# Gate products, rotation, weight splits and gate maxima moved in a hybrid encoder layer

## The chip, the cores and the metric

The kernel runs on one core of a Trainium2 chip. A core has a matrix engine (TensorE, "PE" in the profile, its weight loads "PEld"), VectorE ("DVE"), ScalarE ("ACT"), GpSimd ("POOL") and SyncE ("SP", which here only issues DMAs). Each engine takes its instructions strictly in the order in which they were put into its queue; engines wait for each other through semaphores. TensorE writes only to PSUM, eight banks of 128 x 512 float32; the other engines copy results out of a bank ("evict" it) before TensorE can use it again. GpSimd does not read PSUM in this kernel. The metric is the device time of one execution in microseconds (us), lower is better.

## The reference, cut to what matters

Two sequences (prompt and sample) of 512 tokens with 1024 channels go through one layer with the same weights, in float32:

```python
x = x + 0.5 * swiglu(rms_norm(x), w_gate, w_up, w_down)        # FFN 1, 2816 hidden columns
proj = rms_norm(x) @ w_in                                      # q, k, v, mq, mk, mv, gates, ...
aq, ak = rope(rms_norm(aq)), rope(rms_norm(ak))                # 8 query heads, 2 key heads of 64
att = softmax(aq @ ak.T / 8) @ av
mem = sigmoid(o_pre) * head_norm(mlstm_fwd + mlstm_bwd)        # 4 heads of 128, two directions
x = x + (sigmoid(g_att) * (att @ w_up_att) + sigmoid(g_mlstm) * (mem @ w_up_mlstm)) @ w_out
x = x + 0.5 * swiglu(rms_norm(x), ...)                         # FFN 2, then a final norm

swiglu = (silu(x @ w_gate) * (x @ w_up)) @ w_down
rope:    out[0::2], out[1::2] = x0 * c - x1 * s, x0 * s + x1 * c
mlstm:   D[t, s] = cumsum(f)[t] - cumsum(f)[s] + i[s]          # for s up to t
         m[t] = max(running term, max over s of D[t, s]);  weights exp(D - m);  1 / max(|den|, exp(-m))
```

The mLSTM needs, for each head, direction and block of 128 tokens, the maximum of a gate row: once with a triangular mask added (over s up to t) and once without it (over a whole block). Those maxima fix the scales of all exponentials of the head.

## The kernel before, in words

**Float32 by parts.** Every float32 operand of a matmul is split into a high part (a ScalarE copy, rounded to the format that TensorE takes at full rate) and a low part (a VectorE subtraction, original minus high). A product is then three matmuls: high x high, high x low, low x high. For weights, `fetch_w` issues the DMA into one of four raw buffers (`wr`) and `split_w` (L218 to L223) makes the two parts in one of four buffers (`w8`). `load_w` (L225) is both in a row; it serves the mixing layers.

**FFN, gate and up.** Gate and up weights of 128 hidden columns (a block) and the two sequences form a 2 x 2 by 2 x 2 block product, done with seven products instead of eight; each is twelve matmuls of 512 columns (`product`, L293). There are 22 blocks per FFN. Products accumulate into shared PSUM banks, and sums of them give gate and up of both sequences. `gu_first` does the two products that need only one sequence. For seven blocks it runs ahead and its results are parked in DRAM (`kept`); these blocks later need five products. The order of the blocks alternates a parked with a fresh one for fourteen blocks, then eight fresh ones follow. `gu_rest` (L315 to L347) does the rest of a block: VectorE and ScalarE evict the banks Y and Z (L326, L330, L334, L339, L344), ScalarE applies Silu (L312, L341), and in the last two lines the two products gate x up are formed (L345, L346), on GpSimd. Evictions carry `shifted(SOONER)`. `Sides` (L349 to L378) makes from the results of two blocks the seven right-hand sides of the down projection: splits on ScalarE (L358) and VectorE (L359), differences on VectorE (L365, L372, L374, L376), and two DMAs to DRAM for each (L360, L361). It carries `shifted(LATER)`.

**FFN, down.** `ffn_down` does 28 steps of matmuls (L541) over those sides. The change does not touch it.

**Mixing.** `mix` runs once per sequence. `tok_proj` and `proj` are products with weight slices, each with its own `load_w`; `go` keeps one unit loaded ahead of the one computed. A unit of `proj` is 24 matmuls of 512 columns and one eviction. In order:
1. keys, values and gate columns; then queries.
2. `gates` makes the gate rows and writes them to DRAM (`ebuf`); small columns per block go to `cs`.
3. `rope_apply` (L737 to L758) norms and rotates the keys once and the queries in four blocks: the normed tile times the cosine table on GpSimd (L750), the swapped halves times the sine table on VectorE (L755), the sum on VectorE (L757). `q_rope` splits and transposes the result (L885).
4. Attention, a loop over eight heads: scores and softmax (`scores`, L904, with VectorE's maximum L913, reciprocal L916 and scaling L917 and ScalarE's exponential L915), transposes and product with the values (`attend`, L921), and after each head one or two projection units from `queue` (`fill`).
5. Four mLSTM heads (`mem_head`, L1010, and `mem_out`, L1080), with the value projection (96 matmuls) between the first `mem_head` and its `mem_out` and projection units between the others.
6. Gates, merge and output projection (L1118 to L1138).

In `mem_head`, for each direction, a DMA spreads a gate row from DRAM over all partitions (L1018), GpSimd adds the mask (L1022), VectorE takes the two maxima (L1023, L1024); small VectorE work and one exponential make the scales (L1027 to L1039); then ScalarE makes 20 exponentials of 128 columns (L1061) from the rows with and without mask, and VectorE multiplies them with the scores (L1063). The rows live in four slots (tag `eb`, two per direction), taken in turn.

**Who orders the work.** A planner at compile time turns the program into one queue per engine. Each instruction has a number, its place in the program; among those that the planner takes to be ready by its own estimate of times, the lowest number goes first. `shifted(n)` adds n to the numbers in its block, so a negative n lets them go ahead of earlier code. On the chip the order is fixed: an instruction that waits holds up all behind it on its engine.

Of the kernel before, what the change touches and what calls it, by code (L numbers as in the profile page):

```python
# [8 lines left out]
F32 = mybir.dt.float32  # L9
# [17 lines left out]
def encoder(ctx, tc, I, outs):  # L27
# [14 lines left out]
    def nm(s):  # L42
        n_id[0] += 1
        return f"{s}_{n_id[0]}"
# [173 lines left out]
    def split_w(raw, lo_eng, pin=lambda i: i):  # L218
# [3 lines left out]
        pin(lo_eng.tensor_tensor(lo, raw, f(hi), op=ALU.subtract))  # L222
        return hi, lo  # L223

    def load_w(view, lo_eng):  # L225

        return split_w(fetch_w(view), lo_eng)

# [84 lines left out]
    def gu_rest(W, xc, got, ring, mid):  # L315
# [26 lines left out]
        product(Y, W[T4], xc[T4], False)  # L342
        with shifted(SOONER):
            V_.tensor_tensor(v1, v1, Y, op=ALU.add)  # L344
        G_.tensor_tensor(g0, g0, v1, op=ALU.mult)  # L345
        G_.tensor_tensor(u2, u2, v5, op=ALU.mult)  # L346
        return g0, u2  # L347

    class Sides:  # L349
# [360 lines left out]
    def mix(s, xh, xl, early=None, extra=None, after=None):  # L710
# [4 lines left out]
        def fill(n):  # L715
            go(*queue[:n])
            del queue[:n]
# [19 lines left out]
        def rope_apply(t, rq, tab, bsel):  # L737
# [9 lines left out]
                             rq.unsqueeze(2).to_broadcast([P, 8, DA]), op=ALU.mult)  # L747
            o, m = T2(), T2()
            v4 = lambda x: x.rearrange("p (b h e) -> p b h e", b=nb, e=DA)
            G_.tensor_tensor(v4(o), v4(n), cb, op=ALU.mult)  # L750
            v5 = lambda x: x.rearrange("p (b h i two) -> p b h i two", b=nb, h=hn_, two=2)
            s4 = sb.rearrange("p b (i two) -> p b i two", two=2)
            for bb in range(nb):
# [143 lines left out]
            q_rope(b)  # L897
        go(mem_qk(0, 1), mem_qk(1, 0), mem_qk(1, 1))


        att = A([P, 4, 2, S], F32R, "att")
        afs = {}
# [57 lines left out]
        for h in range(HA):  # L960
            nxt = scores(h + 1) if h + 1 < HA else None
            attend(h, Ps)
            Ps = nxt
            fill(1 if h < 4 else 2)
            if h == 2 and extra:
                extra()
        fill(99)


# [39 lines left out]

        def mem_head(h):  # L1010
            qk = qks[h]
            ebs, ems = [], []
            st = small(64, "st")
            pm_, bm, Mx, mm_, bd, n1, n2, en = [st[:, 8 * i:8 * i + 8].rearrange("p (d b) -> p d b", d=2)
                                               for i in range(8)]
            for d in range(2):
                eb = T2(F32, "eb")
                nc.sync.dma_start(eb, ebuf[d, h:h + 1, :].rearrange("a s -> (a s)").partition_broadcast(P))  # L1018
                em = T2(F32, "eb")
                eb3 = eb.rearrange("p (b s) -> p b s", b=4)  # L1020
                em3 = em.rearrange("p (b s) -> p b s", b=4)
                G_.tensor_tensor(em3, eb3, tabs[3][:, d].unsqueeze(1).to_broadcast([P, 4, P]), op=ALU.add)  # L1022
                V_.tensor_reduce(pm_[:, d], em3, axis=AX.X, op=ALU.max)  # L1023
                V_.tensor_reduce(bm[:, d], eb3, axis=AX.X, op=ALU.max)  # L1024
                ebs.append(eb3)
                ems.append(em3)
            a_, x_, B_ = csv[:, 0, :, :, h], csv[:, 1, :, :, h], csv[:, 2, :, :, h]  # L1027
            V_.memset(Mx[:, :, 0], 0.0)
            for i in range(3):
                V_.tensor_tensor(Mx[:, :, i + 1], Mx[:, :, i], B_[:, :, i], op=ALU.add)  # L1030
                V_.tensor_tensor(Mx[:, :, i + 1], Mx[:, :, i + 1], bm[:, :, i], op=ALU.max)
            V_.tensor_tensor(mm_, a_, Mx, op=ALU.add)
            V_.tensor_tensor(en, pm_, x_, op=ALU.subtract)
            V_.tensor_tensor(mm_, mm_, en, op=ALU.max)
            V_.scalar_tensor_tensor(bd, x_, -1.0, mm_, op0=ALU.mult, op1=ALU.subtract)
            V_.tensor_tensor(n1, a_, mm_, op=ALU.subtract)
            V_.tensor_tensor(n2[:, :, 2:4], n1[:, :, 2:4], B_[:, :, 1:3], op=ALU.add)
            V_.tensor_tensor(n2[:, :, 1], n2[:, :, 3], B_[:, :, 1], op=ALU.add)
            nc.scalar.activation(en, mm_, AF.Exp, scale=-1.0)  # L1039
            dn_ = small(8, "dn")  # L1040
            dn = dn_.rearrange("p (d b) -> p d b", d=2)
            Ts = []
            for i in range(4):
# [5 lines left out]
                for d in range(2):  # L1049
                    W = T2()  # L1050
                    st_ = i if d == 0 else 3 - i
                    for j in range(st_ + 1):
                        b = j if d == 0 else 3 - j
                        if j == st_:
                            src, bias = ems[d][:, j], bd[:, d, st_:st_ + 1]
                        else:
                            src = ebs[d][:, j]
                            dist = st_ - j
                            bias = (n1[:, d, st_:st_ + 1] if dist == 1 else
                                    n2[:, d, st_:st_ + 1] if dist == 2 else n2[:, d, 1:2])  # L1060
                        nc.scalar.activation(W[:, b * P:(b + 1) * P], src, AF.Exp, bias=bias)  # L1061
                    cl = slice(0, (i + 1) * P) if d == 0 else slice(i * P, S)
                    V_.scalar_tensor_tensor(W[:, cl], p[:, cl], DM ** -0.5, W[:, cl], op0=ALU.mult, op1=ALU.mult,  # L1063
                                            accum_out=dn[:, d, st_:st_ + 1])
                    pair.append(W)
                Ts.append(pair)
            V_.scalar_tensor_tensor(dn_, dn_, -1.0, dn_, op0=ALU.mult, op1=ALU.max)
            V_.tensor_tensor(dn, dn, en, op=ALU.max)
            V_.reciprocal(dn_, dn_)
            for i in range(4):  # L1070
                tf, tb = Ts[i]
# [377 lines left out]
```

## Time and profile before

| | us |
|---|---|
| median of three runs (lowest, highest) | 2179.64 (2176.89, 2181.13) |
| profiled execution | 2180.97 |
| its span, first to last instruction | 2179.2 |
| TensorE busy | 2096.6 |
| VectorE busy | 1642.4 |
| ScalarE busy | 954.3 |
| GpSimd busy | 284.3 |
| mean granted TensorE clock | 0.988 of full speed |

How to read the rows in the next section. A row of waits names the engine and line that waited, what it waited for, the total, the number of waits and the longest. A group row has line, engine, operation, result <- operands, shapes and count, then after the bar the busy time in us, the mean in ns, and the idle time before. A timeline row has start, duration, engine, line and operation; in brackets stands how long the engine sat idle before it and for what. Matmuls overlap in TensorE, so their durations add up to more than the time that they take together.

### The profile page before, as it was taken

How to read it: one execution, taken by the hardware profiler on the slowest of the kernel's cores; microseconds unless marked ns; L12 is line 12 of the kernel's file. 1: busy time of each engine (PE TensorE's matmuls, PEld its weight loads, DVE VectorE, ACT ScalarE, POOL GpSimd, SP SyncE). 2: the span in 40 equal slices, each digit the busy share in tenths (PEclk: the TensorE clock that was granted, in tenths of full speed). 3: DMA queues.
4: the chain of work that ended last, by engine and by line, in shares of the span. 5: the costliest groups of instructions: out<-in, count | busy, mean ns of one | idle time of the engine just before them, and what ended most of it. 6: DMA issues, size and time to landing. Idle time of an engine off the chain costs nothing.

```text
span 2179.2 us, 27321 instructions
## 1 busy us (share of the span) xinstructions
PE 2096.6 (96%) x9544; PEld 1707.3 (78%) x9544; DVE 1642.4 (75%) x2881; ACT 954.3 (44%) x1699; POOL 284.3 (13%) x220
## 2 busy tenths in 40 slices
PE   8999999999999999999999999999999999999997
PEld 6877777878888777878887887877777778878886
DVE  7888877776697797785649878766877777776695
ACT  7534443443224466463436664434434344443222
POOL 0111121111002100100121001011111111110002
PEclk9999999999999999999999999999999999999999
DMA  9565654479765122332351233357455544479752
GB/s 298 163 195 183 213 168 157 145 265 382 284 220 181 40 68 57 95 104 77 115 165 39 59 92 95 114 153 224 155 176 171 177 159 159 140 273 386 270 196 106
DMA packets 312473, 366.04 MB, mean 168 GB/s; under 512 B 18352, under 2 KB 208832, under 8 KB 311312
## 3 DMA queue, kind: packets, MB, share of 16 engines
q1 hardware_dynamic: 311744, 363.04, 50.8%
q0 software_dynamic: 592, 1.27, 0.3%
q8 instruction: 75, 1.23, 0.2%
q14 instruction: 62, 0.51, 0.1%
HBM read 255.15 MB, written 109.08 MB: 167 GB/s over the span
## 4 chain that ended last, share of the span: by engine, by line
PE 41%; DVE 7%; issue 4%; ACT 2%; POOL 1%; DMA 1%; DVEq 0%; SPq 0%; ACTq 0%; POOLq 0%
PE mm L707 14%; PE pss L297 5%; PE pst L297 4%; PE mm L541 4%; PE mm L297 2%; PE pss L541 2%; PE pst L541 2%; PE mm L691 2%; PE pso L541 1%; POOL t L346 1%; PE pso L1096 1%; PE pso L936 1%; PE pss L1047 1%; PE pss L910 1%; PE pst L929 1%
## 5 line engine op out<-in xcount | busy, mean ns | idle before, releaser
L707 PE MATMUL mm<-xh,w 128*128 128x512 f32 x896 | 293.4, 397 | 0.0
L297 PE MATMUL pst<-xc,w 128*128 128x512 f32 x1056 | 263.7, 399 | 22.3 <-ACT t L330 22.3
L297 PE MATMUL mm<-xc,w 128*128 128x512 f32 x1056 | 259.6, 393 | 7.0 <-ACT f L306 4.0
L297 PE MATMUL pss<-xc,w 128*128 128x512 f32 x1056 | 256.0, 391 | 3.9 <-DVE t L326 3.9
L297 PEld LDWEIGHTS pst<-xc,w 128*128 128x128 f32 x1056 | 202.6, 193 | 69.9 <-ACT t L330 27.4
L297 PEld LDWEIGHTS mm<-xc,w 128*128 128x128 f32 x1056 | 196.5, 188 | 54.5 <-ACT f L306 7.9
L297 PEld LDWEIGHTS pss<-xc,w 128*128 128x128 f32 x1056 | 197.0, 188 | 48.4 <-DVE t L326 7.7
L707 PEld LDWEIGHTS mm<-xh,w 128*128 128x128 f32 x896 | 167.4, 189 | 32.1
L541 PE MATMUL mm<-rt,w 128*128 128x512 f32 (+1 forms) x819 | 186.0, 383 | 0.2 <-DMA rt<-rbuf 0.2
L221 ACT ACTIVATE w<-wr 128x1024 fp32r<-128x1024 f32 (+1 forms) x112 | 114.7, 1029 | 153.5 <-issue 72.2
L707 PE MATMUL mm<-xl,w 128*128 128x512 f32 x448 | 176.9, 395 | 0.0
L541 PEld LDWEIGHTS mm<-rt,w 128*128 128x128 f32 x819 | 150.2, 188 | 30.4 <-DMA rt<-rbuf 0.6
L346 POOL TENSOR_TENSOR t<-t,t 128x512 f32<-128x512 f32 x44 | 73.1, 1661 | 715.1 <-ACT t L341 547.3
L256 DVE TENSOR_TENSOR w<-t,w 128x512 fp32r<-128x512 f32 x176 | 137.1, 793 | 38.3 <-ACT w L255 36.5
L255 ACT ACTIVATE w<-t 128x512 fp32r<-128x512 f32 x176 | 107.4, 627 | 128.9 <-DVE t L281 42.7
L222 DVE TENSOR_TENSOR w<-wr,w 128x1024 fp32r<-128x1024 f32 (+1 forms) x112 | 137.0, 1224 | 35.1 <-ACT w L221 34.6
L297 PE MATMUL pss<-xc,f 128*128 128x512 f32 x528 | 128.6, 392 | 0.6 <-DVE t L334 0.6
L297 PEld LDWEIGHTS pss<-xc,f 128*128 128x128 f32 x528 | 98.1, 188 | 24.5 <-DVE t L334 4.6
L609 ACT ACTIVATE w<-wr 128x512 fp32r<-128x512 f32 x72 | 44.4, 630 | 132.0 <-PE pso L541 63.6
L609 ACT ACTIVATE w<-t 128x512 fp32r<-128x512 f32 x82 | 51.8, 632 | 110.5 <-PE pst L541 62.3
L541 PE MATMUL pss<-rt,w 128*128 128x512 f32 x396 | 94.5, 390 | 3.4 <-DVE w L610 3.4
L707 PEld LDWEIGHTS mm<-xl,w 128*128 128x128 f32 x448 | 84.7, 189 | 16.2
(328 smaller groups left out, 3896.0 us busy)
## 6 DMA issues: line engine op xcount, KB each, us to landing
rt<-rbuf SPq DMA_DIRECT2D x154, 512.0 KB, 5.9
wr<-in_w_in_dram SPq DMA_DIRECT2D x72, 512.0 KB, 3.9
wr<-in_ffn_w_gate_dram SPq DMA_DIRECT2D x56, 512.0 KB, 4.7
rbuf<-tab SPq DMA_DIRECT2D x90, 256.0 KB, 2.7
wr<-in_ffn_w_up_dram SPq DMA_DIRECT2D x44, 512.0 KB, 4.1
rbuf<-t SPq DMA_DIRECT2D x88, 256.0 KB, 3.3
rbuf<-f SPq DMA_DIRECT2D x66, 256.0 KB, 3.0
rbuf<-R SPq DMA_DIRECT2D x64, 256.0 KB, 2.7
```

The source lines that it names most:

```text
L221: pin(nc.scalar.activation(hi, raw, AF.Copy))
L222: pin(lo_eng.tensor_tensor(lo, raw, f(hi), op=ALU.subtract))
L255: pin(nc.scalar.activation(t[:, 0], src, AF.Copy))
L256: pin(V_.tensor_tensor(t[:, 1], src, f(t[:, 0]), op=ALU.subtract))
L297: nc.tensor.matmul(p, a[:, k, :], xt[:, b, k, :], start=(first and k == 0 and i == 0), stop=(k == HK_ - 1 and i == 2), skip_group_check=True)
L346: G_.tensor_tensor(u2, u2, v5, op=ALU.mult)
L541: nc.tensor.matmul(p, u[:, a, d * P:(d + 1) * P], r[:, b, ts], start=(first and q == 0 and k == 0), stop=(q == len(us) - 1 and k == 2), sk ...
L609: nc.scalar.activation(hi, src, AF.Copy)
L691: nc.tensor.matmul(p[b][:, :N], a[:, k, bs], w_[:, kl, :], start=(k == 0 and i == 0), stop=(k == KD - 1 and i == 2))
L707: nc.tensor.matmul(p, a[:, k, :], b, start=(k == 0 and i == 0), stop=(k == n - 1 and i == 2))
L910: nc.tensor.matmul(p, qT[:, h, b * P:(b + 1) * P], kv[:, hk * 2 + j, :], start=(j == 0), stop=(j == 1))
L929: nc.tensor.transpose(p[:, b * P:(b + 1) * P], Ps[b][:, kb * P:(kb + 1) * P], ident)
```

## The change

Four edits.
- In `gu_rest` the two products gate x up of a block go from GpSimd to VectorE, at the same place of the program.
- In `rope_apply` the product with the cosine table goes from GpSimd to VectorE.
- In `load_w` the split of a weight slice gets a number 60 lower; the fetch keeps its number.
- The maxima of the gate rows are no longer taken in `mem_head`. After each of the eight attention heads `mem_max` loads the row of one of the eight (mLSTM head, direction) pairs, adds the mask and takes the two maxima; after the loop `mem_scales` makes the scales of all heads in one go. `mem_head` loads its rows again and adds the mask again (`mem_rows`), and reads its scales.

```diff
+    WEIGHTS = 60
+
     def load_w(view, lo_eng):
-        return split_w(fetch_w(view), lo_eng)
+        raw = fetch_w(view)
+        with shifted(-WEIGHTS):
+            return split_w(raw, lo_eng)
...
-        G_.tensor_tensor(g0, g0, v1, op=ALU.mult)
-        G_.tensor_tensor(u2, u2, v5, op=ALU.mult)
+        V_.tensor_tensor(g0, g0, v1, op=ALU.mult)
+        V_.tensor_tensor(u2, u2, v5, op=ALU.mult)
...
-            G_.tensor_tensor(v4(o), v4(n), cb, op=ALU.mult)
+            V_.tensor_tensor(v4(o), v4(n), cb, op=ALU.mult)
...
+        st = spool.tile([P, 4, 2, 4, HM], F32, tag="st", bufs=1, name=nm("st"))
+        n1, bd, en, n2 = [st[:, i] for i in range(4)]
+
+        def mem_rows(h, d):
+            eb = T2(F32, "eb")
+            nc.sync.dma_start(eb, ebuf[d, h:h + 1, :].rearrange("a s -> (a s)").partition_broadcast(P))
+            em = T2(F32, "eb")
+            eb3 = eb.rearrange("p (b s) -> p b s", b=4)
+            em3 = em.rearrange("p (b s) -> p b s", b=4)
+            G_.tensor_tensor(em3, eb3, tabs[3][:, d].unsqueeze(1).to_broadcast([P, 4, P]), op=ALU.add)
+            return eb3, em3
+
+        def mem_max(h, d):
+            eb3, em3 = mem_rows(h, d)
+            V_.tensor_reduce(n1[:, d, :, h], em3, axis=AX.X, op=ALU.max)
+            V_.tensor_reduce(bd[:, d, :, h], eb3, axis=AX.X, op=ALU.max)
+
+        def mem_scales():
+            a_, x_, B_ = csv[:, 0], csv[:, 1], csv[:, 2]
+            V_.memset(en[:, :, 0], 0.0)
+            for i in range(3):
+                V_.tensor_tensor(en[:, :, i + 1], en[:, :, i], B_[:, :, i], op=ALU.add)
+                V_.tensor_tensor(en[:, :, i + 1], en[:, :, i + 1], bd[:, :, i], op=ALU.max)
+            V_.tensor_tensor(en, a_, en, op=ALU.add)
...
+            nc.scalar.activation(en, en, AF.Exp, scale=-1.0)
...
             attend(h, Ps)
             Ps = nxt
+            mem_max(h // 2, h % 2)
             fill(1 if h < 4 else 2)
             if h == 2 and extra:
                 extra()
+        mem_scales()
         fill(99)
...
         def mem_head(h):
             qk = qks[h]
-            ebs, ems = [], []
-            st = small(64, "st")
...
-            for d in range(2):
-                eb = T2(F32, "eb")
-                nc.sync.dma_start(eb, ebuf[d, h:h + 1, :].rearrange("a s -> (a s)").partition_broadcast(P))
...
-                G_.tensor_tensor(em3, eb3, tabs[3][:, d].unsqueeze(1).to_broadcast([P, 4, P]), op=ALU.add)
-                V_.tensor_reduce(pm_[:, d], em3, axis=AX.X, op=ALU.max)
-                V_.tensor_reduce(bm[:, d], eb3, axis=AX.X, op=ALU.max)
...
-            nc.scalar.activation(en, mm_, AF.Exp, scale=-1.0)
+            ebs, ems = zip(*[mem_rows(h, d) for d in range(2)])
```

More of the change, by code (lines that the diff above doesn't have):

```diff
@@ L898, in mix @@
         go(mem_qk(0, 1), mem_qk(1, 0), mem_qk(1, 1))
+        st = spool.tile([P, 4, 2, 4, HM], F32, tag="st", bufs=1, name=nm("st"))
[19 more added lines that the diff above has]
+            V_.tensor_tensor(en, a_, en, op=ALU.add)
+            V_.tensor_tensor(n1, n1, x_, op=ALU.subtract)
+            V_.tensor_tensor(en, en, n1, op=ALU.max)
+            V_.scalar_tensor_tensor(bd, x_, -1.0, en, op0=ALU.mult, op1=ALU.subtract)
+            V_.tensor_tensor(n1, a_, en, op=ALU.subtract)
+            V_.tensor_tensor(n2[:, :, 2:4], n1[:, :, 2:4], B_[:, :, 1:3], op=ALU.add)
+            V_.tensor_tensor(n2[:, :, 1], n2[:, :, 3], B_[:, :, 1], op=ALU.add)
+            nc.scalar.activation(en, en, AF.Exp, scale=-1.0)
         att = A([P, 4, 2, S], F32R, "att")
@@ L1011, in mem_head @@
             qk = qks[h]
-            ebs, ems = [], []
-            st = small(64, "st")
-            pm_, bm, Mx, mm_, bd, n1, n2, en = [st[:, 8 * i:8 * i + 8].rearrange("p (d b) -> p d b", d=2)
-                                               for i in range(8)]
-            for d in range(2):
-                eb = T2(F32, "eb")
-                nc.sync.dma_start(eb, ebuf[d, h:h + 1, :].rearrange("a s -> (a s)").partition_broadcast(P))
[L1019 to L1022, printed above, removed]
-                V_.tensor_reduce(pm_[:, d], em3, axis=AX.X, op=ALU.max)
[L1024 to L1038, printed above, removed]
-            nc.scalar.activation(en, mm_, AF.Exp, scale=-1.0)
+            ebs, ems = zip(*[mem_rows(h, d) for d in range(2)])
             dn_ = small(8, "dn")
@@ L1054, in mem_head @@
                         if j == st_:
-                            src, bias = ems[d][:, j], bd[:, d, st_:st_ + 1]
+                            src, bias = ems[d][:, j], bd[:, d, st_, h:h + 1]
                         else:
@@ L1058, in mem_head @@
                             dist = st_ - j
-                            bias = (n1[:, d, st_:st_ + 1] if dist == 1 else
-                                    n2[:, d, st_:st_ + 1] if dist == 2 else n2[:, d, 1:2])
+                            bias = (n1[:, d, st_, h:h + 1] if dist == 1 else
+                                    n2[:, d, st_, h:h + 1] if dist == 2 else n2[:, d, 1, h:h + 1])
                         nc.scalar.activation(W[:, b * P:(b + 1) * P], src, AF.Exp, bias=bias)
@@ L1067, in mem_head @@
             V_.scalar_tensor_tensor(dn_, dn_, -1.0, dn_, op0=ALU.mult, op1=ALU.max)
-            V_.tensor_tensor(dn, dn, en, op=ALU.max)
+            V_.tensor_tensor(dn, dn, en[:, :, :, h], op=ALU.max)
             V_.reciprocal(dn_, dn_)
```

## The prediction, made before the changed kernel ran

> **What bounds the kernel now.** I read the page's first part, then TensorE's waits, then the busy times of stretches, then one stretch of the timeline.
>
> ```profile
> span 2179.2 us, 27321 instructions
> PE 2096.6 (96%) x9544; PEld 1707.3 (78%) x9544; DVE 1642.4 (75%) x2881; ACT 954.3 (44%) x1699; POOL 284.3 (13%) x220
> ```
>
> TensorE is the bound, so an edit is worth only what it takes from TensorE's waits and from its slow clock. The waits (engine, line, what it waited for, us in total, times, longest):
>
> ```profile
> PE pst L297 <- ACT t L330: 22.3, 12, 2.1
> PE pst L885 <- DVE t L610: 6.0, 7, 2.0
> ...
> PE pss L1047 <- DVE t L1063: 3.8, 2, 1.9
> PE pss L910 <- ACT t L915: 2.7, 3, 1.3
> PE mm L707 <- DVE w L222: 2.6, 1, 2.6
> ```
>
> The first row dominates. It lies in the gate and up products, once per pair of a parked and a fresh block, six times in each FFN. The stretches below are cut at such pairs (two of the second FFN and the sum of its six, then the first and last of five in the first FFN). The columns are the stretch, its length, the busy time of TensorE, its weight loads, VectorE, ScalarE and GpSimd, the granted clock, the share of the DMA engines and GB/s:
>
> ```profile
> 1608.96:1645.79 36.83, 34.73 (x146) 28.02 (x145) 28.45 (x41) 14.23 (x24) 6.75 (x4) 0.95 0.53 171
> 1645.79:1681.14 35.35, 33.25 (x146) 26.80 (x145) 28.37 (x41) 14.24 (x24) 6.75 (x4) 1.00 0.55 179
> ...
> sum 218.24, PE 205.64 PEld 165.88 DVE 169.21 ACT 85.61 POOL 41.02; mean PE 34.27 PEld 27.65 DVE 28.20 ACT 14.27 POOL 6.84
> ...
> 112.80:149.50 36.70, 35.20 (x152) 28.43 (x152) 29.40 (x41) 14.87 (x25) 6.24 (x4) 0.98 0.56 177
> ...
> 255.10:290.30 35.20, 33.66 (x150) 27.33 (x149) 29.45 (x41) 14.64 (x25) 6.24 (x4) 1.00 0.60 195
> ```
>
> One product of twelve matmuls takes 2.72 us undisturbed (chain of waits):
>
> ```profile
> 1596.61 2.72 PE mm L297 x12
> ```
>
> A pair has 5 + 7 = 12 products, so 32.64 us of work. Six pairs of the second FFN took 218.24 us, which is 22.4 more than 195.84. Five of the first took 177.5 us (112.80 to 290.30), 14.3 more than 163.2; the few transposes among them are in that excess. So 36.7 us is all that the pairs can give back.
>
> Why the wait is there, from the timeline of one odd block:
>
> ```profile
> 1608.92 0.69 DVE L281 TENSOR_TENSOR t<-t,wr 128x512 f32<-128x512 f32 x1
> 1608.96 1.81 POOL L346 TENSOR_TENSOR t<-t,t 128x512 f32<-128x512 f32 x1 [12.21 <-ACT t L341]
> ...
> 1610.80 0.69 DVE L372 TENSOR_TENSOR t<-t,t 128x512 f32<-128x512 f32 x1 [1.18 <-POOL t L346]
> ...
> 1612.07 0.68 DVE L344 TENSOR_TENSOR t<-t,pss 128x512 f32<-128x512 f32 x1
> ...
> 1612.83 1.67 POOL L345 TENSOR_TENSOR t<-t,t 128x512 f32<-128x512 f32 x1 [2.07 <-DVE t L344]
> ...
> 1613.27 1.77 DVE L256 TENSOR_TENSOR w<-t,w 128x512 fp32r<-128x512 f32 x1
> ...
> 1616.17 0.68 DVE L359 TENSOR_TENSOR tab<-t,tab 128x512 fp32r<-128x512 f32 x1
> 1616.78 0.68 DVE L374 TENSOR_TENSOR t<-t,t 128x512 f32<-128x512 f32 x1
> ...
> 1617.49 0.63 ACT L358 ACTIVATE tab<-t 128x512 fp32r<-128x512 f32 x1 [2.33 <-DVE t L374]
> ...
> 1618.02 0.58 ACT L330 ACTIVATE t<-pst 128x512 f32<-128x512 f32 x1
> ...
> 1618.65 4.62 PE L297 MATMUL pst<-xc,w 128*128 128x512 f32 x12 [2.10 <-ACT t L330]
> ```
>
> The eviction L330 frees the bank that TensorE wants, but on ScalarE it stands behind a copy (L358) that waits for VectorE's L374. VectorE is late for two reasons: L372 sat 1.18 us for GpSimd's multiply, and L256 took 1.77 us instead of 0.69 while L345 ran.
>
> **Edit A, the multiplies on VectorE.** 88 multiplies leave GpSimd and join VectorE. The groups (instructions, then busy us, mean ns):
>
> ```profile
> L345 POOL TENSOR_TENSOR t<-t,t 128x512 f32<-128x512 f32 x44 | 73.8, 1677 | 58.2 <-DVE t L344 58.2
> L256 DVE TENSOR_TENSOR w<-t,w 128x512 fp32r<-128x512 f32 x176 | 137.1, 793 | 38.3 <-ACT w L255 36.5
> L284 DVE TENSOR_TENSOR t<-wr,t 128x512 f32<-128x512 f32 x44 | 41.1, 934 | 0.4
> L281 DVE TENSOR_TENSOR t<-t,wr 128x512 f32<-128x512 f32 x44 | 38.2, 869 | 1.0
> L278 DVE TENSOR_TENSOR t<-wr 128x512 f32<-128x512 f32 x44 | 30.3, 689 | 9.7 <-DMA wr<-in_ffn_w_up_dram 9.6
> ```
>
> L278 is the same shape and hardly stretched, so a multiply costs VectorE 0.69 us: 88 x 0.69 = 60.7 us. Stretching falls away: (793-689) x 176 + (934-689) x 44 + (869-689) x 44 = 18.3 + 10.8 + 7.9 = 37 us. VectorE pays 24 us net over both FFNs. In the pair at 1608.96 two stretched instructions of 1.1 us each go and four multiplies come: 28.45 - 2.2 + 2.8 = 29.0 us, 89% of 32.64. It does not become the bound, but it has little slack.
>
> Now the order above is replayed. L359 to L374 shows starts 0.61 us apart. From L281 at 1608.92 to L374 there are ten VectorE instructions, twelve with the two multiplies. L374 would start at 1608.92 + 11 x 0.61 = 1615.63 and not at 1616.78: 1.15 us sooner, so the wait falls from 2.10 to 0.95. The multiply of u2 waits for the Silu L341; behind it in VectorE's queue stand L372 and L344, whose own inputs are there no sooner, so the wait costs no more than GpSimd's did. Twelve waits x 1.15 = 13.8 us.
>
> The slow clock goes with it. It shows right after the wait of 2.10 us above, and not at the same place of a pair in the first FFN:
>
> ```profile
> 1618.65:1622.07 3.42, 3.42 (x10) 2.75 (x11) 3.42 (x7) 1.51 (x3) 0.00 (x0) 0.65 0.73 282
> ...
> 183.25:186.67 3.42, 3.42 (x15) 2.84 (x16) 3.42 (x7) 1.51 (x3) 0.00 (x0) 1.00 1.00 322
> ```
>
> A pair at clock 0.95 takes 36.83 and one at 1.00 takes 35.35. Four of six pairs are of the first kind: 4 x 1.48 = 5.9. The first FFN's first pair gives 36.70 - 35.20 = 1.5. Replay: 13.8 + 5.9 + 1.5 = 21.2 us. The ends are 36.7 (every wait gone) and a loss: 88 x 0.61 = 53.7 if every multiply held up TensorE. The order will not stay the same: the planner put that copy ahead of L330 expecting it sooner than it came, and with the slow GpSimd steps gone its expectation should fit better. I take -24, a little over the replay. Next late are the remaining 0.95 us and the DMAs that free the output ring.
>
> [...]
>
> **Edit B, rotation.** Ten multiplies go from GpSimd to VectorE.
>
> ```profile
> L750 POOL TENSOR_TENSOR t<-t,tab 128x512 f32<-128x512 f32 x10 | 16.8, 1682 | 50.5 <-DVE t L746 46.5 <-DVE t L610 3.9
> ...
> 736.83 1.85 DVE L755 TENSOR_TENSOR t<-t,tab 128x256 f32<-128x256 f32 x2
> ...
> 753.46 0.75 DVE L755 TENSOR_TENSOR t<-t,tab 128x256 f32<-128x256 f32 x2
> ```
>
> VectorE spent 1.85 us on two products beside GpSimd and 0.75 without it. From the end of the norm to the sum L757 that makes 1.85 before and 0.61 + 0.75 = 1.36 after: 0.5 us a block, eight query blocks, 4 us against TensorE's 6.0 us at L885. Ends: 0 and -6.0. I take -4.
>
> **Edit C, weight splits 60 places sooner.** ScalarE's copy and VectorE's subtraction pass earlier softmax and merge work. The fetch keeps its place, but a raw buffer comes free sooner and with it SP's next fetch.
>
> ```profile
> L222 DVE TENSOR_TENSOR w<-wr,w 128x1024 fp32r<-128x1024 f32 (+1 forms) x112 | 137.0, 1224 | 35.1 <-ACT w L221 34.6
> ```
>
> TensorE waited for it once, 2.6 us; that is the one end. The other is a split of 1.22 us ahead of a softmax reduction in each of the 20 units in the attention stages, +24 if nothing hides it; TensorE had other matmuls in nearly all such places (L910 waited 2.7 us in all). I take -2, near the row of the wait.
>
> **Edit D, maxima during attention.** Sixteen broadcast DMAs and sixteen GpSimd additions are new (each head's rows are loaded twice); the 32 reductions only move, and the small VectorE work on them is done once a layer instead of four times.
>
> ```profile
> L1024 DVE TENSOR_REDUCE st<-box 128x4 f32<-128x512 f32 x16 | 10.9, 680 | 1.7 <-DMA box<-ebuf 1.6
> L1022 POOL TENSOR_TENSOR box<-box,tab 128x512 f32<-128x512 f32 x16 | 22.3, 1395 | 135.7 <-DMA box<-ebuf 135.7
> ...
> 760.00:865.00 105.00, 104.18 (x513) 82.85 (x514) 89.42 (x195) 65.32 (x136) 3.81 (x3) 1.00 0.23 61
> 1165.00:1270.00 105.00, 104.97 (x521) 84.41 (x522) 88.88 (x197) 67.41 (x143) 1.20 (x1) 1.00 0.20 56
> ...
> DMA to landing us min/median/max: 3.2/4.0/4.9
> ```
>
> Gain: a head's exponentials no longer wait for reductions and small steps, at most the 3.8 us of L1047. Cost: in each attention stretch VectorE has 15.6 us free and gets 16 reductions x 0.61 = 9.8 us. A reduction that waits for its addition, and that for its DMA, has the next head's softmax queued behind it, and TensorE behind that. Each DMA also waits on SP for its slot, with weight fetches behind it; four raw buffers cover 4.0 us. The mixer's first head now finds its rows late, but the value projection covers that (96 matmuls, 8 x 2.72 = 21.8 us). Ends: -3.8 and the rival below. I take 0, gain and cost near each other.
>
> **Sum.** -24 - 4 - 2 + 0 = -30 us from the profiled execution's 2180.97 us: 2151. That execution is 1.3 us above the median of 2179.64, so I forecast 2150.
>
> **Rivals.**
> Everything comes back: -36.7 - 6.0 - 2.6 - 3.8 = -49, 2130. For it: the planner's order gets truer; against it: VectorE at 89% in the pairs.
> The wait at L330 stays, because ScalarE's order puts another late copy ahead of it: B to D alone, -6, 2174. For it: `Sides` puts seven copies per pair into that queue; against it: the replay.
> The multiplies stand ahead of evictions: 14 paired blocks x 2 FFNs x 2 = 56 of them x 0.61 = 34 us given back, 2180 at most, no change. Against it: L344 stood behind two other instructions here, and among the long waits of this stage is none for it.
> Slower: VectorE fills up in attention. Eight additions a layer block it as L345 did (1.1 us each, 8.8) beside the 9.8, together 18.6 over 15.6 free; from there each head's softmax is late by 1.1 + 2 x 0.61 = 2.3 us. 16 heads: 37 us, and a slow clock of 1.48 after two in three: 16. With A to C: 2150 + 53 = 2203. Against it: the reductions have no deadline before the last head, and L1024's mean of 680 ns shows reductions that GpSimd's additions did not stretch.
>
> **Chances.** Forecast 0.52 (its own range 2138 to 2162), everything 0.18, wait stays 0.14, evictions 0.05, attention 0.11. A measurement of this kernel can't tell less than about 0.2% (4.4 us) from no change. Faster: 0.52 + 0.18 + two thirds of 0.14 = 0.79; same: the rest of 0.14 and 0.05, 0.10; slower 0.11. The range takes in the first four, 2126 to 2182.
>
> **What would show it.** A: waits of TensorE for L330's eviction at most 1 us each, clock 1.00 in the pairs, pair times of 33 to 34 us, VectorE near 29.0 us a pair, L284's mean back at 0.69. B: the rotation's pair of products at 0.75 us and under 3 us of TensorE's wait for the turned queries. C: no wait of the output projection for a split. D: the additions at 32, TensorE's wait for the first mixing matmuls gone, VectorE near 98 of 105 us in attention. Waits for exponentials of the scores in most heads would prove the slower rival; waits of 2 us at L330 would prove the forecast wrong.

## The result and the profile after

The changed kernel takes 2142.2 us (2135.74 to 2144.9), the kernel before beside it 2178.26: a ratio of 0.983, 95% interval 0.980 to 0.985. That is 36 us less; the forecast was 30 less, 2150, with 2138 to 2162 as its own range. The profiled execution has a span of 2143.1 us. The first part of the profile after:

```profile
span 2143.1 us, 27234 instructions
PE 2084.7 (97%) x9544; PEld 1699.1 (79%) x9544; DVE 1633.9 (76%) x2895; ACT 957.6 (45%) x1693; POOL 145.4 (7%) x138
```

TensorE is still the bound and does the same 9544 matmuls. VectorE took over 98 multiplies from GpSimd and is busy for 8.5 us less than before (1642.4). Up to L900 the lines of the changed kernel have numbers four higher than before (38 higher in attention, 13 behind it): the eviction of Z is now L334, the addition before it L330. TensorE's waits in the changed kernel (engine, line, what it waited for, us in total, times, longest):

```profile
PE pss L301 <- DVE t L330: 9.2, 11, 1.8
...
PE pst L889 <- DVE t L614: 4.5, 4, 1.8
...
PE pss L948 <- ACT t L953: 2.3, 5, 0.8
...
PE mm L711 <- DVE ml L614: 1.3, 1, 1.3
PE mm L711 <- ACT mh L613: 1.2, 1, 1.2
```

The largest wait of before, 22.3 us for the eviction of Z, has no row any more. The largest is now 9.2 us for the addition L330.

To see where the time went, I cut both kernels at the same work: from one eviction of Z to another, counted from the first block that is finished. The four stretches are five pairs of the first FFN (evictions 2 to 12), the rest of its blocks (12 to 22), five pairs of the second FFN (24 to 34) and the rest of its blocks (34 to 44). Columns as in the prediction's stretches. The kernel before:

```profile
94.58:272.13 177.55, 169.35 (x737) 136.95 (x736) 145.68 (x200) 72.49 (x123) 31.71 (x20) 0.99 0.58 188
272.13:468.03 195.90, 189.45 (x833) 153.91 (x832) 145.68 (x204) 81.30 (x138) 37.77 (x25) 1.00 0.50 164
1565.29:1747.90 182.61, 172.11 (x721) 138.91 (x720) 142.37 (x201) 71.18 (x120) 33.76 (x20) 0.96 0.53 171
1747.90:1937.94 190.04, 186.91 (x817) 152.60 (x816) 141.73 (x204) 79.88 (x132) 34.20 (x20) 1.00 0.47 158
```

The changed kernel:

```profile
95.35:265.89 170.54, 168.12 (x737) 135.48 (x736) 139.81 (x219) 72.92 (x124) 0.00 (x0) 1.00 0.60 192
265.89:453.59 187.70, 187.70 (x833) 154.43 (x832) 149.36 (x227) 82.49 (x137) 0.00 (x0) 1.00 0.53 178
1544.31:1715.52 171.21, 166.03 (x721) 133.97 (x720) 140.56 (x220) 71.46 (x120) 0.00 (x0) 1.00 0.54 176
1715.52:1903.61 188.09, 186.34 (x817) 152.62 (x816) 147.91 (x228) 81.71 (x133) 0.00 (x0) 1.00 0.50 170
```

The four changes are -7.0, -8.2, -11.4 and -2.0 us, together -28.6 of the 36.1 by which the spans differ (2179.2 to 2143.1). The ten pairs give 18.4 of it. (The first five begin one block sooner than the forecast's five.) The blocks behind them give 10.2; the forecast's sixth pair of the second FFN lies in the last stretch, but for most of the second stretch's 8.2 us it had no term.

The eviction itself now stands ahead of the recombination's last copies. ScalarE at the same eviction of the changed kernel (the 27th of 44, at 1618.02 before):

```profile
1588.93 0.63 ACT L362 ACTIVATE tab<-t 128x512 fp32r<-128x512 f32 x1 [0.93 <-DVE t L349]
1591.84 0.60 ACT L334 ACTIVATE t<-pst 128x512 f32<-128x512 f32 x1 [2.28 <-PE pst L301]
...
1593.38 0.62 ACT L362 ACTIVATE tab<-t 128x512 fp32r<-128x512 f32 x1
```

Before, L330 stood behind a copy that had waited 2.33 us for VectorE. Now that copy comes after the eviction; ScalarE waits for TensorE (2.28 us) and evicts as soon as the product is there.

### The profile page after: what moved, and what is told of

The parts are those of the page before. It is cut to its first block, busy times and chain, and to the rows that moved or that the text cites. A ratio compares the mean times of both kernels' runs of the same rounds, so it can differ in the third digit from the quotient of the medians.

```text
span 2143.1 us, 27234 instructions
## 1 busy us (share of the span) xinstructions
PE 2084.7 (97%) x9544; PEld 1699.1 (79%) x9544; DVE 1633.9 (76%) x2895; ACT 957.6 (45%) x1693; POOL 145.4 (7%) x138
## 4 chain that ended last, share of the span: by engine, by line
PE 79%; DVE 10%; DMA 6%; ACT 3%; issue 2%; SPq 0%; POOL 0%; DVEq 0%; ACTq 0%; POOLq 0%
PE mm L711 17%; PE pss L301 14%; PE pst L301 8%; PE mm L545 8%; PE mm L301 8%; PE pss L545 4%; PE pst L545 4%; PE mm L695 4%; PE pso L545 3%; DMA wr<-in_ffn_w_up_dram 2%; DMA rbuf<-t 1%; PE pso L974 1%; PE pso L695 1%; PE pst L967 1%; PE pss L948 1%
## 5 line engine op out<-in xcount | busy, mean ns | idle before, releaser
L301 PE MATMUL pst<-xc,w 128*128 128x512 f32 x1056 | 255.4, 390 | 0.0
L301 PEld LDWEIGHTS pss<-xc,w 128*128 128x128 f32 x1056 | 196.5, 188 | 56.1 <-DVE t L330 15.7
L301 PEld LDWEIGHTS pst<-xc,w 128*128 128x128 f32 x1056 | 197.3, 188 | 43.2 <-ACT t L334 2.5
L221 ACT ACTIVATE w<-wr 128x1024 fp32r<-128x1024 f32 (+1 forms) x112 | 114.6, 1029 | 166.7 <-issue 61.0
L260 DVE TENSOR_TENSOR w<-t,w 128x512 fp32r<-128x512 f32 x176 | 118.3, 688 | 40.4 <-ACT w L259 37.4
L545 PE MATMUL pst<-rt,w 128*128 128x512 f32 x396 | 93.7, 389 | 0.0
```

The source lines that it names most:

```text
L221: pin(nc.scalar.activation(hi, raw, AF.Copy))
L260: pin(V_.tensor_tensor(t[:, 1], src, f(t[:, 0]), op=ALU.subtract))
L301: nc.tensor.matmul(p, a[:, k, :], xt[:, b, k, :], start=(first and k == 0 and i == 0), stop=(k == HK_ - 1 and i == 2), skip_group_check=True)
L545: nc.tensor.matmul(p, u[:, a, d * P:(d + 1) * P], r[:, b, ts], start=(first and q == 0 and k == 0), stop=(q == len(us) - 1 and k == 2), sk ...
```

## The experiments

Every kernel was compared with the kernel before on the same chip; several chips were used, so two rows are best compared by their ratios. A table of the medians, and the lengths of the four stretches (first pairs, rest; second pairs, rest), cut in each profile at the same evictions:

| kernel | median us | ratio to before, 95% | four stretches, us | sum |
|---|---|---|---|---|
| before | 2177.0 to 2179.6 | 1 | 177.6, 195.9, 182.6, 190.0 | 746.1 |
| changed | 2142.2 | 0.983 (0.980 to 0.985) | 170.5, 187.7, 171.2, 188.1 | 717.5 |
| A alone (a_only) | 2145.0 | 0.984 (0.983 to 0.986) | 169.7, 187.4, 170.7, 187.6 | 715.4 |
| changed without A (no_a) | 2174.3 | 0.998 (0.997 to 1.000) | 177.2, 198.2, 182.1, 190.1 | 747.6 |
| half of A: u2 (half_u2) | 2152.5 | 0.988 (0.987 to 0.990) | 172.8, 190.5, 170.7, 186.4 | 720.4 |
| half of A: g0 (half_g0) | 2163.2 | 0.993 (0.991 to 0.995) | 173.3, 196.9, 171.5, 188.7 | 730.4 |
| blocking put back (lock) | 2153.1 | 0.989 (0.988 to 0.991) | 171.2, 191.3, 177.2, 189.4 | 729.0 |
| before, no delay (before_later0) | 2173.9 | 0.998 (0.997 to 1.000) | 180.2, 192.9, 179.0, 190.2 | 742.2 |
| changed without B (no_b) | 2144.3 | 0.985 (0.984 to 0.987) | | |
| changed without C (no_c) | 2139.6 | 0.983 (0.982 to 0.985) | | |
| changed without D (no_d) | 2139.9 | 0.983 (0.981 to 0.985) | | |
| maxima twice (max_twice) | 2149.5 | 0.987 (0.985 to 0.989) | | |
| T1 sent first (t1_first) | 2134.0 | 0.979 (0.978 to 0.981) | 169.0, 187.7, 166.7, 185.3 | 708.7 |
| changed, no delay (later0) | 2133.5 | 0.979 (0.978 to 0.981) | 167.4, 187.5, 167.4, 186.5 | 708.8 |

### Which edit it is

a_only, the kernel before with edit A:

```diff
-        G_.tensor_tensor(g0, g0, v1, op=ALU.mult)
-        G_.tensor_tensor(u2, u2, v5, op=ALU.mult)
+        V_.tensor_tensor(g0, g0, v1, op=ALU.mult)
+        V_.tensor_tensor(u2, u2, v5, op=ALU.mult)
```

> The kernel before with edit A alone (both gate products of a block on VectorE). Theory: the gate and up stages hold the larger part of the gain. In the two traces TensorE's time over the undisturbed pace of its matmuls fell by about 28 us there and by about 8 us in the mixing layers, so this kernel should be 28 us faster than before, near 2150 us, with no wait for the eviction of Z in the pairs. Rival: the gain comes from the mixing edits and from a planner's order that is better by chance; then this kernel gains under 10 us.

no_a, the changed kernel with the same two lines back on GpSimd:

```diff
-        V_.tensor_tensor(g0, g0, v1, op=ALU.mult)
-        V_.tensor_tensor(u2, u2, v5, op=ALU.mult)
+        G_.tensor_tensor(g0, g0, v1, op=ALU.mult)
+        G_.tensor_tensor(u2, u2, v5, op=ALU.mult)
```

> The changed kernel with edit A undone (gate products back on GpSimd; rotation, splits and maxima as changed). Theory: the gate and up stages are as before, with twelve waits of up to 2.1 us for the eviction of Z, and only the 8 us of the mixing layers are kept: 2170 us. Rival: 2150 us or less, if the mixing edits carried the gain.

A alone gives 2145.0, 33.8 us less than before; without A the other three edits give 4 us or so. TensorE's wait for Z's eviction comes back in no_a just as it was:

```profile
PE pst L301 <- ACT t L334: 22.4, 12, 2.1
```

So A is nearly the whole of it, and it is larger than the 24 us of the forecast.

### What in A: two halves, blocking alone, order alone

half_u2 and half_g0 are the kernel before with only one of the two multiplies moved:

```diff
-        G_.tensor_tensor(u2, u2, v5, op=ALU.mult)
+        V_.tensor_tensor(u2, u2, v5, op=ALU.mult)
```

> The kernel before with only the product u2 x v5 on VectorE; g0 x v1 stays on GpSimd. Theory (replay in the order of before): VectorE no longer sits 1.18 us for GpSimd ahead of the difference for T3 and pays 0.61, so the copy ahead of the eviction of Z comes some 0.6 us sooner; the wait falls to 1.5 us and the slow clock goes: 12 x 0.6 + 7.4 = 15 us faster, 2164. Rival: GpSimd's other product still blocks VectorE once per block and is the later of the two, so this half alone gains nothing: 2178.

```diff
-        G_.tensor_tensor(g0, g0, v1, op=ALU.mult)
+        V_.tensor_tensor(g0, g0, v1, op=ALU.mult)
```

> The kernel before with only the product g0 x v1 on VectorE; u2 x v5 stays on GpSimd. Theory (replay): one block of 1.08 us on VectorE goes and 0.61 is paid, 0.5 us sooner: 12 x 0.5 + 7.4 = 13 us faster, 2165. Rival: this product is the last input of T2 and T4, so it alone holds the chain and this half gains nearly all, 25 us or more: 2153.

TensorE's waits for the two evictions with u2 moved, and then with g0 moved:

```profile
PE pss L297 <- DVE t L326: 7.3, 8, 1.3
...
PE pst L297 <- ACT t L330: 5.6, 5, 1.1
```

```profile
PE pst L297 <- ACT t L330: 13.3, 12, 1.2
PE pss L297 <- DVE t L326: 6.3, 6, 3.6
```

u2 alone gains 26 us by the medians, far more than the 15 of its theory; g0 alone gains 15.5, near its 13. With g0 moved every pair still waits, but at most 1.2 us and not 2.1. The halves do not add up: over the four stretches they give 25.7 and 15.7 us, both together 30.7. The reason is in the five pairs of the second FFN. Here is that stretch with g0 moved:

```profile
1564.10:1735.56 171.46, 165.66 (x721) 134.05 (x720) 137.46 (x212) 71.20 (x120) 17.09 (x10) 1.00 0.57 182
```

It took 182.61 us before, at a clock of 0.96; now it takes 171.46 at 1.00. The same 721 matmuls kept TensorE busy for 172.11 us and then for 165.66: 6.5 of the 11.2 us are the slow clock, the rest is five waits shortened by 0.9 us. Either half of A is enough to win back nearly the whole of this stretch (170.7 and 171.5 us, against 170.7 with both), so the second half can't win it again.

lock is the changed kernel with two squares on GpSimd behind the products, over values that nobody reads again:

```diff
         V_.tensor_tensor(g0, g0, v1, op=ALU.mult)
         V_.tensor_tensor(u2, u2, v5, op=ALU.mult)
+        G_.tensor_tensor(v1, v1, v1, op=ALU.mult)
+        G_.tensor_tensor(v5, v5, v5, op=ALU.mult)
```

> The changed kernel; after each of the two gate products GpSimd squares in place the operand that is dead by then (v1 and v5), 88 multiplies that nobody reads. Nothing of the output depends on them. Theory: what GpSimd took from the block was both the time of its product on the way to the copy and the blocking of VectorE. Blocking alone stretches some 40 VectorE instructions by 1.1 us each but leaves the chain without GpSimd's 1.7 us: 10 to 15 us slower than the changed kernel, 2155. Rival one: blocking is nearly all of it, and the time is that of before, 2170 or more. Rival two: VectorE has slack for it, 2145.

TensorE's first wait and two groups of VectorE (busy us, mean ns) in lock:

```profile
PE pss L301 <- DVE t L330: 15.3, 13, 2.5
```

```profile
L260 DVE TENSOR_TENSOR w<-t,w 128x512 fp32r<-128x512 f32 x176 | 126.9, 737 | 28.0 <-ACT w L259 25.1
L288 DVE TENSOR_TENSOR t<-wr,t 128x512 f32<-128x512 f32 x44 | 38.5, 875 | 0.3
```

Nobody computes with GpSimd's results here, and still 11.5 us of the 28.6 in the four stretches are lost again (717.5 to 729.0), 10.9 us in the medians. By the ratios it is 14 us. (The squares are written over v1 and v5, so the buffers come free later than in the changed kernel too; how much of this is due to that, no run separates.) Nor is the blocking quite that of the kernel before: in gate and up 56 of VectorE's operations are stretched, by 42 us in all, and before it was 52, by 49 us, partly at other lines. What remains of A, some 20 us, I put down to the chain itself, VectorE and ScalarE waiting for results that took 1.7 us; that part was only argued, since no run has slow results without the blocking.

before_later0 leaves all multiplies on GpSimd and takes away the delay of the recombinations, so that the order changes and nothing else:

```diff
-    LATER, SOONER = 100,-100
+    LATER, SOONER = 0, -100
```

> The kernel before, with all its multiplies on GpSimd, and the delay of the deferred work (the recombinations) set from 100 places to none. That edit alone took 9 us from the changed kernel. Theory (the slow multiplies on GpSimd and the VectorE instructions stretched beside them make VectorE late, and no place in the queue mends that): TensorE's wait for the eviction of Z, 22.3 us in 12 places, stays at 1 us or more in most pairs, and the time is 2160 to 2185. Rival (the copies of the recombination stand ahead of that eviction only through this delay, so the order alone is the cause): the wait is gone, and the time is 2150 or less without any multiply moved.

```profile
PE pss L297 <- DVE t L326: 13.1, 10, 1.8
PE pst L297 <- ACT t L330: 10.3, 12, 2.1
```

The wait for Z's eviction halves, to 0.9 us on average in the same twelve places, which is a little less than the theory asked for; but 13.1 us of waits for the addition L326 come (3.9 before), and the time hardly moves: 5.7 us less by the medians, 4 by the ratio, whose interval reaches from 0 to 7. Order alone does not do it while GpSimd is in the chain.

### What is late now

t1_first is the changed kernel with T1 sent ahead of T3, so that a slot of the ring "h" is read out sooner:

```diff
             V_.tensor_tensor(b12, b22, b12, op=ALU.subtract)
-            self.out(T3, b12, True)
             V_.tensor_tensor(b22, b22, t1, op=ALU.subtract)
             self.out(T1, t1, True)
+            self.out(T3, b12, True)
```

> The changed kernel with one step of the recombination moved: the subtraction b22 -= t1 and the sending of T1 go ahead of the sending of T3, so that the slot of the output ring is read out sooner. In the changed kernel TensorE waited 9.2 us in 11 places for the addition L330, which in the longest of them waited 2.22 us for the transfer out of that slot. Theory (that transfer is the last wait left in the pairs): the wait for L330 falls from 9.2 to under 3 us, TensorE's own time is the same, and the median is some 5 us under the changed kernel's, near 2137. Rival (VectorE's order is the limit there, and the transfer was merely the last to end): the waits move to another addition or eviction, the total of TensorE's waits in the two gate and up stages changes by less than 2 us, and the time stays at 2142.

The wait in the changed kernel (timeline):

```profile
1600.02 0.69 DVE L330 TENSOR_TENSOR t<-t,pss 128x512 f32<-128x512 f32 x1 [2.22 <-DMA rbuf<-t]
1600.76 3.93 PE L301 MATMUL pss<-xc,w 128*128 128x512 f32 x16 [1.83 <-DVE t L330]
```

TensorE's wait for the same addition in t1_first:

```profile
PE pss L301 <- DVE t L330: 2.0, 3, 0.9
```

L330 writes u2 into one of the five slots of the ring "h". T1's low part is made in place in such a slot, and L330 waits until its DMA has read it. With T1 sent sooner the row falls from 9.2 to 2.0 us, VectorE's own longest wait for that transfer from 2.2 to 0.9, and nothing takes its place. By the medians the kernel is some 8 us faster than the changed one: 2134.0 against 2142.2. The two intervals touch at 0.980 to 0.981, and 8 is rather the upper end: the changed kernel was profiled in the longest of its four executions, and in the five other kernels with the same gate and up code (a_only, no_b, no_c, no_d, max_twice) the four stretches add up to 714.0 to 716.2 us, against 708.7 here.

later0 makes the edit of before_later0 in the changed kernel:

```diff
-    LATER, SOONER = 100,-100
+    LATER, SOONER = 0, -100
```

> The changed kernel with the delay of the deferred work in gate and up set from 100 places to none, so that the recombinations and the split of the gate rows are no longer held back behind the evictions. Theory (the gain comes from the evictions standing early in VectorE's and ScalarE's queues; the order set by this delay keeps them there): TensorE waits again for evictions in each pair, 1 to 2 us for each of 12, and the time is 10 to 25 us longer than the changed kernel's, 2152 to 2167. Rival (with the multiplies off GpSimd the evictions come in time in any order): the waits of TensorE in the pairs stay under 1 us and the time is within 4 us of 2142.

```profile
PE pss L301 <- DVE t L330: 2.5, 4, 1.3
```

Here my theory fell. I expected the evictions to come late again and 10 to 25 us to be lost; instead the kernel is as fast as t1_first, and by the same wait: the rival had the waits right, and its time of 2142 was too long. Without GpSimd in the chain the evictions come in time in either order, and I take it that with no delay the recombination's DMAs go out sooner and free the slot (VectorE sat idle at L330 for that transfer for 7.7 us in the changed kernel and 1.9 here); the order of the DMAs by itself was not tried in this kernel. So the delay was no help in either kernel. Taking it away gains 5.7 us by the medians while GpSimd is in the chain and 8.7 once it is not (4 and 8 by the ratios); the intervals are too wide to tell the two apart.

### B, C and D

no_b puts the rotation's product back on GpSimd, no_c sets the 60 places of C to 0, no_d is the kernel before with A, B and C. The diffs stand against the changed kernel.

```diff
-            V_.tensor_tensor(v4(o), v4(n), cb, op=ALU.mult)
+            G_.tensor_tensor(v4(o), v4(n), cb, op=ALU.mult)
```

> The changed kernel with edit B undone (rotation's cosine product back on GpSimd). Theory: TensorE's waits for the turned queries go from 4.5 us back to about 6 us or more and the blocked sine products to 1.85 us a pair; 2 to 4 us slower than the changed kernel, 2145. Rival: with the additions of edit D also on GpSimd around the rotation, more than 5 us: 2148 or above.

```diff
-    WEIGHTS = 60
+    WEIGHTS = 0
```

> The changed kernel with edit C undone (a weight split has the number of its place again). Theory: the 2.6 us wait of the output projection for a split comes back with its slow clock, 2 to 4 us slower than the changed kernel, 2145. Rival: nothing, since the changed kernel waits there for the merged tiles instead (2.5 us): 2142.

```diff
-            mem_max(h // 2, h % 2)
...
-        mem_scales()
...
         def mem_head(h):
-            ebs, ems = zip(*[mem_rows(h, d) for d in range(2)])
+            ebs, ems = [], []
...
```

> The kernel before with edits A, B and C, without D (maxima stay in the memory heads). Theory: the two waits of 2 us of the first mixing matmuls of a head come back, and the attention stages lose the 7 us of VectorE's work each; near no difference to the changed kernel, at most 4 us slower: 2142 to 2146. Rival: D costs more in attention than it gives, and this kernel is faster than the changed one by 3 us or more: 2139.

None of the three differs from the changed kernel by more than the intervals allow, so what follows is read from profiles and not from times. Without B TensorE waits longer for the turned queries (4.5 us in the changed kernel):

```profile
PE pst L889 <- DVE t L614: 7.2, 6, 2.4
```

Without C the one wait of the output projection for a split is there again:

```profile
PE mm L711 <- DVE w L222: 2.6, 1, 2.6
```

But the changed kernel has two waits at the same line, 1.3 and 1.2 us, for the two parts of the merged operand: C removed a wait behind which another stood. The attention stretches without D, and then those of the changed kernel:

```profile
745.00:850.00 105.00, 104.42 (x513) 83.42 (x512) 90.83 (x197) 67.30 (x142) 5.83 (x5) 1.00 0.22 61
1148.00:1253.00 105.00, 104.77 (x516) 83.96 (x515) 89.23 (x196) 67.12 (x138) 5.39 (x4) 1.00 0.22 61
```

```profile
745.00:850.00 105.00, 102.71 (x504) 81.42 (x505) 96.63 (x203) 65.60 (x137) 10.48 (x8) 1.00 0.26 73
1148.00:1253.00 105.00, 103.94 (x513) 82.88 (x512) 96.19 (x206) 68.05 (x144) 10.35 (x8) 1.00 0.25 72
```

D puts VectorE up by some 6 us in each, and TensorE does 1.7 and 0.8 us less work in them. Against that stands the wait for the first mixing matmuls, which no_d still has and the changed kernel has not:

```profile
PE pss L1049 <- DVE t L1065: 3.6, 2, 2.1
...
PE pst L887 <- DVE t L612: 1.6, 2, 1.0
```

The wait for the turned queries is 1.6 us without D and 4.5 with it, which eats up most of what B gained. The traces show a part of the reason. In the prompt's first block of queries two of D's additions run beside the two products with the sine table, which then take 2.94 us together; without D the same two take 0.76:

```profile
721.27 2.85 POOL L914 TENSOR_TENSOR box<-box,tab 128x512 f32<-128x512 f32 x2 [27.90 <-DMA box<-ebuf]
721.47 2.94 DVE L759 TENSOR_TENSOR t<-t,tab 128x256 f32<-128x256 f32 x2
```

```profile
718.90 0.76 DVE L757 TENSOR_TENSOR t<-t,tab 128x256 f32<-128x256 f32 x2
```

Behind this block TensorE waits 1.75 us for the turned queries, and in no_d not at all.

max_twice takes every one of D's reductions twice, with the same result:

```diff
             V_.tensor_reduce(bd[:, d, :, h], eb3, axis=AX.X, op=ALU.max)
+            V_.tensor_reduce(n1[:, d, :, h], em3, axis=AX.X, op=ALU.max)
+            V_.tensor_reduce(bd[:, d, :, h], eb3, axis=AX.X, op=ALU.max)
```

> The changed kernel with both reductions of every head taken twice: 32 reductions more on VectorE in the attention stages, some 20 us of VectorE work there, with the same result. It measures how near VectorE is to the bound in attention after the change, where it was busy 96 of 105 us. Theory (the reductions have no deadline and fill VectorE's idle time; that idle time is nearly used up): the first 16 us or so go into the idle time of the two stages, 16 to 18 us in all, and what does not fit lies on TensorE's path: 0 to 6 us more than the changed kernel, 2142 to 2148. Slower rival of the prediction (each reduction delays the next head's softmax): each of 16 heads is later by two reductions of 0.61 us, 1.2 us, 20 us more with waits for the exponentials of the scores in most heads: 2162, and more with the slow clock.

The first attention stretch of max_twice, and TensorE's wait for the exponentials there:

```profile
745.00:850.00 105.00, 100.87 (x486) 78.76 (x485) 99.52 (x202) 61.09 (x122) 11.83 (x9) 0.98 0.26 75
```

```profile
PE pss L950 <- ACT t L955: 6.1, 8, 1.5
```

It costs 7.3 us by the medians (the interval just touches the changed kernel's), a little over the theory's 6 and far from the rival's 20. VectorE reaches 99.5 of 105 us, and TensorE now waits 6.1 us for the exponentials in eight places (2.3 us in five places in the changed kernel). In the changed kernel VectorE has some 17 us free in the two stretches, so 32 reductions 0.61 us apart, nearly 20 us, no longer fit.

## Why the prediction was right, point by point

**The bound and the place of the gain: right.** TensorE's waits and slow clock in gate and up were what could be had, and A took them; B to D did little.

**A's cause: right, with two shares.** GpSimd's late results and the stretched VectorE instructions made the eviction late. lock shows the blocking alone worth 11 to 14 us of A's 34, with the reservations above; before_later0 shows 4 to 6 us for another order alone. The rest is argued.

**A's size: mis-sized twice, in opposite ways.** The step that failed is the sentence that 36.7 us "is all that the pairs can give back", used as the end of A's term. It counted eleven pairs and stopped there. Cut at evictions around these eleven (3 to 13 and 24 to 36), a_only gave 7.3 + 13.7 = 21.0 us: less than the 24 taken, and the replay's 21.2. Beyond them it gave 9.7 us that the sum had nothing for: 2.3 at the first pair of the first FFN, which was not among the eleven, 6.8 in the rest of that FFN's blocks and 0.6 in the rest of the second's. Before, TensorE waited among those blocks too, behind the pairs of the first FFN (290 to 480 us):

```profile
PE pss L297 <- DVE t L326: 3.1, 3, 1.9
PE mm L297 <- ACT t L306: 1.2, 2, 0.9
PE pss L297 <- DVE t L334: 0.6, 1, 0.6
```

In a_only the same blocks show no wait. I had read the waits by their largest row alone and cut my stretches where that row was. A lies in the four stretches with 30.7 us. Another 4.2 us lie between the last eviction of the first FFN and the first of the second, where A moves next to nothing: there the kernel before has five stretches of 3.41 us at half clock and a_only three, an estimate of 3.4 us.

**The total: partly luck.** A came out 10 us above its term, and B to D together at some 2 us (36.1 less 33.8) and not 6. The two errors have opposite signs, which brings 30 near to 36.

**The replay of the order: failed in form.** It kept the old order and left 0.95 us of wait at each eviction of Z. The planner's order changed, as the text allowed for, and the eviction stands ahead of the copy: that wait is gone wholly. What TensorE waits for in its place is the addition L330 and, behind it, the slot: 9.2 us in eleven places. "Next late are ... the DMAs that free the output ring" named it, without a price; t1_first gives the price as 5 to 8 us.

**The slow clock: right, and the sum's 5.9 us was close.** It went with the waits: 6.5 us in the five pairs of half_g0. In the pairs the kernel before has five stretches of 3.41 us at half clock and the changed kernel none, an estimate of 5 x 1.7 = 8.5 us against the forecast's 5.9 + 1.5.

**VectorE in the pairs: cost overrated.** The forecast was 29.0 us a pair. The first and the last of six pairs of the second FFN, and their mean, in the changed kernel:

```profile
1530.68:1565.72 35.04, 34.31 (x152) 27.92 (x151) 28.66 (x45) 14.72 (x25) 0.00 (x0) 1.00 0.56 178
...
1703.00:1736.56 33.56, 33.20 (x144) 26.80 (x145) 28.11 (x44) 14.46 (x24) 0.00 (x0) 1.00 0.57 187
sum 205.88, PE 200.34 PEld 161.88 DVE 169.22 ACT 86.81 POOL 0.00; mean PE 33.39 PEld 26.98 DVE 28.20 ACT 14.47 POOL 0.00
```

A pair takes 33.6 to 35.0 us (33 to 34 forecast) and VectorE 28.2, just as before. The forecast let three groups shrink back, 37 us. They did (L260 at 688, L285 at 688, L288 at 686 ns), but the splits of the recombination had been stretched too, by some 12 us more, and I left them out. The largest change among them, before and after:

```profile
L359 DVE TENSOR_TENSOR tab<-t,tab 128x512 fp32r<-128x512 f32 x17 | 15.0, 880 | 5.7 <-ACT tab L358 5.5
```

```profile
L363 DVE TENSOR_TENSOR tab<-t,tab 128x512 fp32r<-128x512 f32 x17 | 11.6, 685 | 0.9 <-ACT tab L362 0.7
```

**B: the mechanism right, the gain hardly kept.** The products with the sine table went back to 385 ns from 546 on average, and to 319 without D; TensorE's wait fell by the forecast's 4 us only without D (5.7 us in a_only, 1.6 in no_d, which has C as well). The forecast had not asked what D's additions would do beside the rotation.

**C: wrong by its 2 us.** The wait it removed covered two others.

**D: right at 0.** VectorE reached 96.6 of the 98 us forecast, the additions are 32, the wait for the first mixing matmuls is gone, and the stage paid about as much.

**The rivals.** "Everything comes back" was half true (-36 of -49); t1_first went to 2134. "The wait at L330 stays" and "ahead of evictions" did not happen: among TensorE's waits after there is no row for VectorE's eviction behind the multiplies (L348). "Attention" did not happen, and its price of 2.3 us for each of 16 heads was too high: 32 reductions on top of D's cost 7.3 us, not 37.

## What to carry to other kernels

When a slow engine's results feed the engine that evicts, price the move over the whole stage in which the slow engine runs, all waits together, and not over the places of the largest wait. After such a move try the ordering hints again that the old kernel had: here, taking away a delay gave some 8 us, and my theory said that it would cost 10 to 25. And a removed wait is worth the distance to the next one at the same place: C's 2.6 us had 2.5 behind it.

## What the runs showed of the hardware

**Half clock followed stretches of 3.41 us in which TensorE was idle for 1.8 to 2.5 us.** The traces of the kernel before and of the changed kernel record the granted clock as 1.00 or 0.50; from 30 to 2110 us each record of 0.50 is 3.41 us long (one of the kernel before 6.83). I cut both traces into stretches of 3.41 us, with these records on their borders. Here is the stretch of the kernel before that holds the wait of 2.10 us, and the next one; then, of the changed kernel, the two stretches that share the wait of 1.83 us, and the next one:

```profile
1616.28:1619.69 3.41, 1.31 (x6) 0.86 (x5) 3.38 (x6) 2.20 (x5) 0.00 (x0) 1.00 0.95 350
1619.69:1623.10 3.41, 3.41 (x9) 2.65 (x8) 3.30 (x6) 0.47 (x1) 0.00 (x0) 0.50 0.69 245
```

```profile
1596.40:1599.81 3.41, 2.53 (x12) 1.75 (x10) 1.40 (x3) 0.90 (x2) 0.00 (x0) 1.00 0.86 312
1599.81:1603.22 3.41, 2.46 (x11) 2.04 (x12) 1.38 (x2) 0.63 (x1) 0.00 (x0) 1.00 0.59 177
1603.22:1606.64 3.42, 3.42 (x16) 2.63 (x15) 2.82 (x5) 0.86 (x2) 0.00 (x0) 1.00 0.05 19
```

In the first case TensorE was busy for 1.31 of 3.41 us, 38%, and the next stretch ran at half clock. In the second the wait fell on both sides of a border, TensorE was busy for 2.53 and 2.46 us, and the clock stayed. A wait of 1.78 us in the same kernel, ended at 1509.58, lay within one stretch (1507.65 to 1511.06), left TensorE busy for 1.63 us, 48%, and the half clock followed. All stretches at full clock from 30 to 2110 us, counted in these two traces: in the kernel before nine of 598 were followed by half clock, and in them TensorE was busy for 26 to 44%; of the other 589 the lowest had 45%, the next 50%. In the changed kernel it was three of 605, with 26, 28 and 48%; the lowest of the others had 54%. The waits in the pairs with g0 moved, 1.16 us on average, leave TensorE busy for 66% of a stretch (an estimate, 2.25 of 3.41 us), and there the clock stayed at 1.00. Of the six pairs of the second FFN before, all with a wait of 2.1 us, four ran at 0.95 and two at 1.00: in the four it left TensorE busy for 38% of a stretch, in the two for 51 and 58%. What sets the clock the traces do not show. In that time the kernel before has ten stretches at half clock and the changed kernel three, an estimate of 7 x 1.7 = 12 of the 36 us.

**GpSimd's additions stretch VectorE's softmax scaling too.** It multiplies a tile by one value per partition. Its mean was 481 ns before (L917) and 495 without D (L919), and with D's additions in the attention loop it is 523. Five of the 64 take 862 to 1510 ns, each beside one of the additions (L914); no other takes more than 489:

```profile
L955 DVE TENSOR_SCALAR t<-t,asm 128x512 f32<-128x512 f32 x64 | 33.4, 523 | 0.2
```

That is 42 ns x 64 = 2.7 us more than before, which the forecast had not counted.
